# Fully filled warming products, a later first norm, weights split three pieces ahead, and last rows in two halves: a two-layer encoder on one core

## The chip, the cores and the metric

The kernel runs on one core of a Trainium2 chip. The times are device microseconds of that core for the whole kernel, one launch: the median of some runs, with the lowest and the highest. A profile is one execution of its own, taken by the hardware profiler; its span runs from its first to its last instruction or transfer, and the time of that execution is a little longer than its span.

The engines are TensorE (PE; its weight loads are listed apart as PEld), VectorE (DVE), ScalarE (ACT), GpSimd (POOL) and SyncE (SP), which only issues transfers here. Each works through its own list of instructions in order and waits on semaphores for the others. DMA transfers are issued from SP's queue and, for a few, from ACT's (ACTq in the profile).

## The reference

Two layers (DEPTH = 2) over x of 512 tokens by 1024 features, float32. Cut to what matters:

```python
for l in range(DEPTH):
    h = rms_norm(x, attn_norm_g[l])
    proj = h @ w_in[l]
    c_q, c_kv, k_rope, gq, gk, gv, pool_in, gate_logits = split_columns(proj, IN_SIZES)
    o_mla = mla_branch(c_q, c_kv, k_rope, ...)       # 8 heads, low-rank q and kv, rotary key, per-head norms
    o_gqa = gqa_branch(gq, gk, gv, ...)              # 8 heads of 64, 2 key/value heads, per-head norms, rotary
    o_pool = pool_branch(pool_in, w_pool[l], ...)    # means over 2/4/8/16 tokens minus the token, linear per group
    gates = sigmoid(gate_logits).reshape(b, s, 3, d)
    merged = (gates[:, :, 0] * (o_mla @ w_branch_mla[l])
              + gates[:, :, 1] * (o_gqa @ w_branch_gqa[l])
              + gates[:, :, 2] * (o_pool @ w_branch_pool[l]))
    x = x + merged @ w_out[l]
    hf = rms_norm(x, ffn_norm_g[l])
    u = depthwise_conv(hf @ ffn_w_up[l], ...)        # width 3, 2 x 2816 channels
    u_gate, u_val = u[..., :D_FF], u[..., D_FF:]
    x = x + (silu(u_gate) * u_val) @ ffn_w_down[l]
```

## The kernel before

**Layout and products.** Activations stand feature-major: `XM` is 128 partitions x 8 blocks (KC) x 512 tokens, the running x; `HH` and `HL` are the high and low parts of x times the norm's gain. A float32 product is made of three: high by high, high by low, low by high (`mm3`, L351 on, through the helper `mm`, L343; the profile lists nearly all products under L344). Results gather in PSUM banks with tags: two `acc`, two `ST`, two `AV`, one `mi`, one `S`. `ps(tag)` takes a bank and `free(tag)` gives it back when the evacuating operation is recorded.

**Weights.** One stream of weights comes from HBM in transfers of up to 128 x 1024 (`w_dma`, L298, on SP's queue, three raw buffers; the first eight go to general slots). Each is used in pieces of up to 512 columns. `w_split` (L305) makes a piece's high part `wh` by a copy on ACT (L208) and its low part `wl` by a subtraction (L215). Pieces 0 to 7 have that subtraction on DVE; after that `pick` (L320) takes DVE or POOL, whichever is free first by the plan. `wnext` (L336) hands out piece j and has pieces up to j + LA split first (LA = 2, `hlp` has LA + 2 buffers of each part). In `make_q` (L889 on), which takes two pieces and uses them over four token blocks, `st["la"]` cuts this to LA - 1.

**The order.** The order on each engine is written by the program itself: a `Clock` keeps a planned time, PE's work moves it forward, and `chain(...)` puts a row of steps for the other engines on a heap, each due when the one before it should end or when the key that it needs is ready. At run time each engine follows the order so recorded. In the attentions a `Filler` puts other products (gates, branch projections, `make_q`) between the score products of the heads.

**Stages of a layer.** `tok_major` makes the latents and the rotary key token-major: eight blocks by four banks by three products of 384 columns, 96 products, and consumes pieces 0 to 7 in layer 0. Then `norm_finish` (L438) sums the squares `sq` over the partitions with eight small products by `ones` into a bank `S` (in fp32, two columns each), makes the reciprocal root `rt` on DVE and POOL and the diagonal tiles `dg`; the latents' evacuation waits for `rt`. `feat_major` makes one block of 128 features by 512 tokens, 8 x 3 products; the four pooled groups come first, and after group 0 `norm_rows` (L461) spreads the norm over all partitions (`rbc`). After that follow keys and values, the two attentions, the merged branches (accumulated on DVE into `XM`, which is saved to `xsp` and loaded again), the output projection, the second norm, the feed-forward's up-projections (44 blocks) and down-projections (8 blocks of 66 products each).

**The attention's queries.** `t_pair` (L1060 on) transposes two heads into bank `mi`, then copies each head's half to `qa` (`hi`), subtracts it into the other half of `qa`, and makes a second copy `qb <- qa` of 64 x 512 (`lo`). `copy` (L470) picks ACT or DVE by the plan. The exponentials are on ACT (`ps_ST <- ps_ST`), the probabilities' parts are `ph` (a copy) and `pl` (a subtraction on DVE).

**Slots.** Nearly all other tiles of 128 x 528 floats come from one pool `sp` of 53 slots.

**Start and end.** PE begins with 18 products of `ones` by `ones`, 128 columns each (L1407). Squares of x are made by ACT (`square`) and summed by DVE (`sum_up`) beside `tok_major`. At the end, each of the eight blocks of the last down-projection is added to `XM` by DVE (128 x 512) and sent to `out` by SP.

Of the kernel before, what the change touches and what calls it, by code (L numbers as in the profile page):

```python
# [13 lines left out]
AF = mybir.ActivationFunctionType  # L14
# [4 lines left out]
P = 128  # L19
T = 512  # L20
# [8 lines left out]
SLOT = 528  # L29
NSLOT = 53  # L30
RAW = 3
# [3 lines left out]
PRE_B = 17  # L35
LA = 2
END = object()
# [209 lines left out]
def trunk(ctx: ExitStack, tc: tile.TileContext, x, w, prm, gb, cst, out):  # L247
# [8 lines left out]
    rawp = ctx.enter_context(tc.tile_pool(name="rawp", bufs=RAW))  # L256
    hlp = ctx.enter_context(tc.tile_pool(name="hlp", bufs=LA + 2))
    sp = ctx.enter_context(tc.tile_pool(name="sp", bufs=NSLOT))
# [35 lines left out]
    soff = np.concatenate([[0], np.cumsum(swidth)]) * P  # L294
    st = {"dma": 0, "split": 0, "use": 0, "la": LA}
    raws, halves = {}, {}
# [8 lines left out]
    def w_split():  # L305
        j = st["split"]
        sl, off, wd = pieces[j]
        r = raws[sl][:, off:off + wd]
        hi = hlp.tile([P, T], F32R, tag="wh", name=f"wh{j}")
        lo = hlp.tile([P, T], F32R, tag="wl", name=f"wl{j}")  # L310
        ck.fin = ck.now
        A.activation(hi[:, :wd], r, AF.Copy)
        e = V if j < KC else pick(W_BIAS, ck.fin + ck.SEM)
        ck.free[e.kind] = max(ck.free.get(e.kind, 0.0), ck.fin + ck.SEM)
        e.tensor_tensor(lo[:, :wd], r, f(hi[:, :wd]), ALU.subtract)
        done("w", j)
        halves[j] = (hi, lo)
        st["split"] += 1
# [17 lines left out]
    def wnext():  # L336
        j = st["use"]
        w_ahead(j + st["la"] if j > LA else j)
        st["use"] += 1
        need(("w", j))  # L340
        return halves.pop(j)
# [168 lines left out]
    def layer(l, sq, xsrc):  # L510
# [66 lines left out]
        tok_major(latb, 384)  # L577
        norm_finish(G1, sq, nrm)
        rt = nrm["rt"]

        def rtok(b):
            return rt[:, 2 * b:2 * b + 1]

# [15 lines left out]
        def lat_norm():  # L599
            for b in range(4):  # L600
# [3 lines left out]

        chain(*[([("rt", G1)], lambda b=b: lat_evac(b)) for b in range(4)], lat_mean,
              *rsqrt_steps(ssc.rearrange("p a b -> p (a b)"), 8, ("ssc", l)), lat_norm)

# [46 lines left out]
        for g in range(4):  # L654
            acc = ps(ptags[g])
            run(feat_major(acc, G1))
            if g == 0:
                norm_rows(G1, nrm, "acc")
            chain(*pool_steps(g, acc, ptags[g]))
# [59 lines left out]
        def gq_token():  # L719
            s_ = ssr[:, 0:32].rearrange("p (b h) -> p b h", b=4)  # L720
            V.tensor_tensor(s_, s_, bc(rt.rearrange("p (b t) -> p b t", t=2)[:, :, 0:1], [P, 4, 8]), ALU.mult)

# [166 lines left out]
        def make_q(g):  # L889
            ws = (wnext(), wnext())  # L890
            st["la"] = LA - 1
            for b in range(4):
# [8 lines left out]
                q_out(g, b, acc)  # L901
            st["la"] = LA
            if g == 1:
# [128 lines left out]
        def attention(kind, fill, okey, odst):  # L1032
# [27 lines left out]
            def t_pair(h):  # L1060
# [7 lines left out]
                for i in range(2):  # L1068
# [8 lines left out]
                    def lo(i=i, qa=qa, qb=qb, own=own, other=other):  # L1077
                        V.tensor_tensor(qa[other, :T], tp[own], f(qa[own, :T]), ALU.subtract)
                        if i == 1:
                            free("mi")  # L1080
                        copy(qb[0:64, :T], qa[own, :T], False)
                        done(*key("q", h + i))
# [290 lines left out]
        sq = None if last else slot("sq")  # L1373
        idx = 0
        for m in range(KC):
            tag = tags[m % 3]
            acc = ps(tag)
            for kc in range(FC):
# [4 lines left out]
                idx += 1  # L1383
                mm3(acc, wh[:, ws], wl[:, ws], act[kc][0][:, :T], act[kc][1][:, :T], kc == 0, kc == FC - 1)

# [19 lines left out]
    idle = ps("mi")  # L1405
    for _ in range(18):
        PE.matmul(idle[:, :P], lhsT=ones, rhs=ones, start=True, stop=True)  # L1407
    free("mi")
# [161 lines left out]
```

## Time and profile before

| | us |
|---|---|
| median of 3 runs | 1654.65 |
| lowest and highest | 1654.59, 1656.44 |
| the profiled execution | 1653.45 |
| its span | 1651.6 |
| PE busy in the span | 1643.0 (99%) |
| DVE, ACT, POOL busy | 885.7, 770.0, 929.5 |
| waits of the PE over all, by the profile | 4.5 |

How to read the profile: times are from the span's start. A row of the timeline has the start, the duration, the engine, the line of the kernel, the operation, output and inputs, shapes, a count where equal operations are joined, and in brackets how long the engine stood idle before and what ended that. A matmul's duration reaches from its start until its result is through, so that consecutive ones overlap; the pace is read from the distance of their starts. A row of the waits has the waiting operation, what it waited for, the sum of the idle time, the number of waits and the longest. A row with min/median/max gives the durations in ns of one operation by its shape.

### The profile page before, as it was taken

To read this page: it belongs to the slowest core of one execution; us is meant where nothing else is said; L and a number is where in the kernel's file an instruction comes from. 1 tells how busy PE (TensorE), PEld (TensorE's weight loads), DVE (VectorE), ACT (ScalarE), POOL (GpSimd) and SP (SyncE) were. 2 spreads that over 40 slices of the span, in tenths; PEclk is the share of its full clock that TensorE was granted. 3 is DMA by queue.
4 is the path that set the end of the run, shared out by engine and by line. 5 is a ranking of instruction groups with operands and counts; after the bars stand their busy time and mean duration, and the time that the engine had idled before them with its cause. 6 is when DMAs were issued, how large, how long until landed. Compare 5 with 4: busy or idle time off the path is not lost.

```text
span 1651.6 us, 20235 instructions
## 1 busy us (share of the span) xinstructions
PE 1643.0 (99%) x7378; PEld 1334.5 (81%) x7378; DVE 885.7 (54%) x1395; ACT 770.0 (47%) x1361; POOL 929.5 (56%) x809
## 2 busy tenths in 40 slices
PE   9999999999999999999999999999999999999999
PEld 8887887778888888888888878877788888888887
DVE  6677756643356666620046677566332666667000
ACT  6357755553444444432244577455434444444221
POOL 4762764344666566555568528634446656656543
PEclk9999999999999999999999999999999999999999
DMA  5231121124323323333333212211243223222331
GB/s 189 80 96 36 58 74 52 39 64 135 107 90 90 102 89 92 100 107 110 110 101 91 85 32 62 74 52 38 84 128 109 89 91 101 90 96 96 113 110 58
DMA packets 44595, 145.40 MB, mean 88 GB/s; under 512 B 5072, under 2 KB 6352, under 8 KB 44496
## 3 DMA queue, kind: packets, MB, share of 16 engines
q1 hardware_dynamic: 44352, 144.10, 27.7%
q8 instruction: 58, 0.95, 0.2%
q14 instruction: 41, 0.34, 0.1%
q10 hardware_dynamic: 144, 0.01, 0.0%
HBM read 139.90 MB, written 4.19 MB: 87 GB/s over the span
## 4 chain that ended last, share of the span: by engine, by line
PE 97%; DVE 1%; ACT 1%; DMA 0%; issue 0%; SPq 0%; DVEq 0%
PE ps_acc L344 43%; PE ps_AV L344 24%; PE ps_ST L344 24%; PE ps_S L344 3%; PE ps_mi L344 2%; PE ps_mi L348 1%; DVE sq L215 0%; DMA XM<-x 0%; ACT HH L208 0%; PE ps_acc L348 0%; SPq L301 0%; SPq L1410 0%; ACT wh L208 0%; DVE vmh L231 0%; DVE qa L215 0%
## 5 line engine op out<-in xcount | busy, mean ns | idle before, releaser
L215 POOL TENSOR_TENSOR wl<-raw,wh 128x512 fp32r<-128x512 f32 (+3 forms) x512 | 670.7, 1318 | 590.3 <-ACT wh L208 512.9
L208 ACT ACTIVATE wh<-raw 128x512 fp32r<-128x512 f32 (+3 forms) x522 | 314.9, 608 | 185.4 <-PE ps_ST L344 82.5
L219 DVE SCALAR_TENSOR_TENSOR a<-u,prm,a 128x512 f32<-128x512 f32 x176 | 240.6, 1368 | 79.4 <-ACT a L208 70.0
L344 PE MATMUL ps_acc<-HH,wh 128*128 128x512 f32 x592 | 234.8, 397 | 1.9 <-DVE XM L219 1.8
L344 PE MATMUL ps_acc<-HH,wl 128*128 128x512 f32 x592 | 234.2, 396 | 0.6 <-POOL wl L215 0.6
L344 PE MATMUL ps_acc<-HL,wh 128*128 128x512 f32 x592 | 233.6, 395 | 0.0
L344 PEld LDWEIGHTS ps_acc<-HH,wh 128*128 128x128 f32 x592 | 111.3, 188 | 28.5 <-ACT mqs L208 2.1
L344 PEld LDWEIGHTS ps_acc<-HH,wl 128*128 128x128 f32 x592 | 111.2, 188 | 27.9 <-POOL wl L215 1.1
L344 PEld LDWEIGHTS ps_acc<-HL,wh 128*128 128x128 f32 x592 | 111.3, 188 | 26.0
L208 ACT ACTIVATE ps_ST<-ps_ST 128x512 f32<-128x512 f32 x128 | 74.5, 582 | 115.6 <-PE ps_ST L344 115.2
L344 PE MATMUL ps_AV<-HH,wl 128*128 128x512 f32 x288 | 114.2, 397 | 0.0
L223 DVE TENSOR_REDUCE nm<-ps_S 128x1 fp32r<-128x512 f32 x128 | 87.8, 686 | 49.2 <-PE ps_S L344 48.0
L344 PE MATMUL ps_AV<-HH,wh 128*128 128x512 f32 x288 | 114.0, 396 | 0.0
L344 PE MATMUL ps_AV<-HL,wh 128*128 128x512 f32 x288 | 113.3, 393 | 0.0
L215 DVE TENSOR_TENSOR pl<-ps_ST,ph 128x512 fp32r<-128x512 f32 x128 | 87.7, 686 | 39.5 <-ACT ph L208 38.2
L215 POOL TENSOR_TENSOR al<-a,ah 128x512 fp32r<-128x512 f32 x44 | 58.1, 1321 | 84.8 <-ACT ah L208 64.6
L344 PE MATMUL ps_ST<-HH,wl 128*128 128x512 f32 x240 | 95.1, 396 | 0.0
L344 PE MATMUL ps_ST<-HH,wh 128*128 128x512 f32 x240 | 95.1, 396 | 0.0
L344 PE MATMUL ps_ST<-HL,wh 128*128 128x512 f32 x240 | 94.4, 393 | 0.0
L208 ACT ACTIVATE a<-u,prm 128x512 f32<-128x512 f32 x88 | 71.7, 815 | 31.3 <-DVE u L215 31.1
L208 ACT ACTIVATE ah<-a 128x512 fp32r<-128x512 f32 x44 | 27.8, 631 | 117.0 <-DVE u L243 111.4
L208 ACT ACTIVATE a<-a 128x512 f32<-128x512 f32 x44 | 27.8, 632 | 114.1 <-DVE u L243 114.1
(347 smaller groups left out, 3518.1 us busy)
## 6 DMA issues: line engine op xcount, KB each, us to landing
raw<-w SPq DMA_DIRECT2D x228, 512.0 KB, 3.5
raw<-w SPq DMA_DIRECT2D x13, 384.0 KB, 3.1
XM<-x SPq DMA_DIRECT2D x16, 256.0 KB, 3.9
raw<-w SPq DMA_DIRECT2D x6, 448.0 KB, 3.4
xsp<-XM SPq DMA_DIRECT2D x8, 256.0 KB, 2.0
XM<-xsp SPq DMA_DIRECT2D x8, 256.0 KB, 3.4
out<-XM SPq DMA_DIRECT2D x8, 256.0 KB, 2.0
raw<-w SPq DMA_DIRECT2D x4, 432.0 KB, 3.1
```

Of the source, the lines that this page charges most:

```text
L208: return self.eng.activation(out, in_, func, **k)
L215: return self.eng.tensor_tensor(out, *a)
L219: return self.eng.scalar_tensor_tensor(out, *a)
L223: return self.eng.tensor_reduce(out, in_, *a, **k)
L344: PE.matmul(o, lhsT=lhsT, rhs=rhs, start=start, stop=stop)
L348: PE.transpose(o, src, ident)
```

## The change

It has five parts.

1. The 18 warming products of 128 columns become 9 of 512 columns (the right operand repeats `ones` four times).
2. In layer 0 `norm_finish` and the latents' chain are recorded after the fourth of the eight blocks of pooled group 0 (12 of its 24 products), no longer ahead of it; `norm_rows` comes after group 1, no longer after group 0. Layer 1 keeps its order.
3. LA is 3: pieces are split three ahead and `hlp` has six buffers of each part. `make_q` no longer cuts this. Pieces 8, 9 and 10 have their subtraction on DVE for certain. To make room the pool of slots has 49.
4. The second copies `qb <- qa` are always on ACT.
5. In the last layer's last block of the down-projection, the 512 tokens are made in two halves of 256 columns, in banks `mi` and `S`. For the first 19 of 22 blocks both halves are computed in turn; then half 0 gets its last three blocks, its addition and its transfer (SP) are recorded, and half 1 gets its last nine products, its addition and a transfer from ACT's queue. These are 132 products of 256 columns in place of 66 of 512, two additions of 128 x 256 and two transfers of 128 KB.

```diff
--- before.py
+++ after.py
@@ -27,13 +27,13 @@
 FC = D_FF // P
 WINDOWS = (2, 4, 8, 16)
 SLOT = 528
-NSLOT = 53
+NSLOT = 49
 RAW = 3
 EXTRA = (("q", 2, (2, 5)), ("n", 2, (6, 7)), ("v", 1, (0, 3)))
 PRO = 0.47
 PRE_A = 16
 PRE_B = 17
-LA = 2
+LA = 3
 END = object()
 RSQRT_BITS = 1597463007.0
 SLACK = 35
@@ -254,7 +254,7 @@
 
     cp = ctx.enter_context(tc.tile_pool(name="cp", bufs=1))
     rawp = ctx.enter_context(tc.tile_pool(name="rawp", bufs=RAW))
-    hlp = ctx.enter_context(tc.tile_pool(name="hlp", bufs=LA + 2))
+    hlp = ctx.enter_context(tc.tile_pool(name="hlp", bufs=LA + 3))
     sp = ctx.enter_context(tc.tile_pool(name="sp", bufs=NSLOT))
     sm = ctx.enter_context(tc.tile_pool(name="sm", bufs=2))
     pp = ctx.enter_context(tc.tile_pool(name="pp", bufs=1, space=PSUM))
@@ -292,7 +292,7 @@
 
     pieces, swidth = _stream()
     soff = np.concatenate([[0], np.cumsum(swidth)]) * P
-    st = {"dma": 0, "split": 0, "use": 0, "la": LA}
+    st = {"dma": 0, "split": 0, "use": 0}
     raws, halves = {}, {}
 
     def w_dma():
@@ -310,7 +310,7 @@
         lo = hlp.tile([P, T], F32R, tag="wl", name=f"wl{j}")
         ck.fin = ck.now
         A.activation(hi[:, :wd], r, AF.Copy)
-        e = V if j < KC else pick(W_BIAS, ck.fin + ck.SEM)
+        e = V if j < KC + 3 else pick(W_BIAS, ck.fin + ck.SEM)
         ck.free[e.kind] = max(ck.free.get(e.kind, 0.0), ck.fin + ck.SEM)
         e.tensor_tensor(lo[:, :wd], r, f(hi[:, :wd]), ALU.subtract)
         done("w", j)
@@ -335,7 +335,7 @@
 
     def wnext():
         j = st["use"]
-        w_ahead(j + st["la"] if j > LA else j)
+        w_ahead(j + LA if j > LA else j)
         st["use"] += 1
         need(("w", j))
         return halves.pop(j)
@@ -575,11 +575,11 @@
         ltags = ("acc", "acc", "ST", "ST")
         latb = [ps(t) for t in ltags]
         tok_major(latb, 384)
-        norm_finish(G1, sq, nrm)
-        rt = nrm["rt"]
+        if l:
+            norm_finish(G1, sq, nrm)
 
         def rtok(b):
-            return rt[:, 2 * b:2 * b + 1]
+            return nrm["rt"][:, 2 * b:2 * b + 1]
 
         mx = [slot("mx") for _ in range(4)]
         ssc = small("ssc", [P, 4, 2])
@@ -602,8 +602,12 @@
                 V.tensor_scalar(mx[b][:, 256:384], mx[b][:, 256:384], ssc[:, b, 1:2], None, ALU.mult)
             done("lat", l)
 
-        chain(*[([("rt", G1)], lambda b=b: lat_evac(b)) for b in range(4)], lat_mean,
-              *rsqrt_steps(ssc.rearrange("p a b -> p (a b)"), 8, ("ssc", l)), lat_norm)
+        def latents():
+            chain(*[([("rt", G1)], lambda b=b: lat_evac(b)) for b in range(4)], lat_mean,
+                  *rsqrt_steps(ssc.rearrange("p a b -> p (a b)"), 8, ("ssc", l)), lat_norm)
+
+        if l:
+            latents()
 
 
         mixed = {}
@@ -653,8 +657,11 @@
         ptags = ("AV", "AV", "mi", "S")
         for g in range(4):
             acc = ps(ptags[g])
-            run(feat_major(acc, G1))
-            if g == 0:
+            for n, _ in enumerate(feat_major(acc, G1)):
+                if l == 0 and g == 0 and n == 3:
+                    norm_finish(G1, sq, nrm)
+                    latents()
+            if g == (l == 0):
                 norm_rows(G1, nrm, "acc")
             chain(*pool_steps(g, acc, ptags[g]))
 
@@ -718,7 +725,7 @@
 
         def gq_token():
             s_ = ssr[:, 0:32].rearrange("p (b h) -> p b h", b=4)
-            V.tensor_tensor(s_, s_, bc(rt.rearrange("p (b t) -> p b t", t=2)[:, :, 0:1], [P, 4, 8]), ALU.mult)
+            V.tensor_tensor(s_, s_, bc(nrm["rt"].rearrange("p (b t) -> p b t", t=2)[:, :, 0:1], [P, 4, 8]), ALU.mult)
 
         def gq_norm(b):
             o = gqo[b][:, :T].rearrange("p (h f) -> p h f", f=64)
@@ -888,7 +895,6 @@
 
         def make_q(g):
             ws = (wnext(), wnext())
-            st["la"] = LA - 1
             for b in range(4):
                 if b:
                     yield
@@ -899,7 +905,6 @@
                     lh, ll = lat[kc]
                     mm3(acc[:, :384], lh[:, bs], ll[:, bs], wh[:, :384], wl[:, :384], kc == 0, kc == 1)
                 q_out(g, b, acc)
-            st["la"] = LA
             if g == 1:
                 chain(([("ssq", l, i, b) for i in range(2) for b in range(4)],
                        lambda: G.tensor_scalar(ss[:, 0], ss[:, 0], 1.0 / 96, EPS, ALU.mult, ALU.add)),
@@ -1078,7 +1083,7 @@
                         V.tensor_tensor(qa[other, :T], tp[own], f(qa[own, :T]), ALU.subtract)
                         if i == 1:
                             free("mi")
-                        copy(qb[0:64, :T], qa[own, :T], False)
+                        A.activation(qb[0:64, :T], qa[own, :T], AF.Copy)
                         done(*key("q", h + i))
 
                     steps.append((hi, lo))
@@ -1371,7 +1376,18 @@
 
         last = l == L - 1
         sq = None if last else slot("sq")
-        idx = 0
+        idx, tail = 0, []
+        two = [ps(t) for t in ("mi", "S")] if last else None
+
+        def half(n, kc, wh, wl):
+            ts = slice(256 * n, 256 * n + 256)
+            mm3(two[n][:, :256], wh, wl, act[kc][0][:, ts], act[kc][1][:, ts], kc == 0, kc == FC - 1)
+
+        def out_half(n):
+            ts = slice(256 * n, 256 * n + 256)
+            V.tensor_tensor(XM[:, KC - 1, ts], two[n][:, :256], XM[:, KC - 1, ts], ALU.add)
+            (SY, nc.scalar)[n].dma_start(out[KC - 1][:, ts], XM[:, KC - 1, ts])
+
         for m in range(KC):
             tag = tags[m % 3]
             acc = ps(tag)
@@ -1381,7 +1397,20 @@
                 need(("act", l, kc))
                 ws = slice((idx % 4) * P, (idx % 4) * P + P)
                 idx += 1
-                mm3(acc, wh[:, ws], wl[:, ws], act[kc][0][:, :T], act[kc][1][:, :T], kc == 0, kc == FC - 1)
+                if not (last and m == KC - 1):
+                    mm3(acc, wh[:, ws], wl[:, ws], act[kc][0][:, :T], act[kc][1][:, :T], kc == 0, kc == FC - 1)
+                elif kc < FC - 3:
+                    half(0, kc, wh[:, ws], wl[:, ws])
+                    half(1, kc, wh[:, ws], wl[:, ws])
+                else:
+                    half(0, kc, wh[:, ws], wl[:, ws])
+                    tail.append((kc, wh[:, ws], wl[:, ws]))
+            if tail:
+                chain(lambda: out_half(0))
+                for z in tail:
+                    half(1, *z)
+                chain(lambda: out_half(1))
+                continue
 
             def resid(m=m, acc=acc, tag=tag):
                 V.tensor_tensor(XM[:, m, :], acc, XM[:, m, :], ALU.add)
@@ -1403,8 +1432,8 @@
     A.activation(warm, warm, AF.Exp)
     V.memset(f(ones), 1.0)
     idle = ps("mi")
-    for _ in range(18):
-        PE.matmul(idle[:, :P], lhsT=ones, rhs=ones, start=True, stop=True)
+    for _ in range(9):
+        PE.matmul(idle, lhsT=ones, rhs=ones[:, None, :].to_broadcast([P, 4, P]), start=True, stop=True)
     free("mi")
     for kc in range(KC):
         SY.dma_start(XM[:, kc, :], x[kc])
```

## The prediction

> **What bounds the kernel now.** I read the page first, then the PE's waits, then the timeline around every place where the PE stood still. The page (busy us, share of the span, instructions; then the chain that ended last) and, as third line, the last row of the chain's own list (start, us, engine, tile, count):
>
> ```profile
> PE 1643.0 (99%) x7378; PEld 1334.5 (81%) x7378; DVE 885.7 (54%) x1395; ACT 770.0 (47%) x1361; POOL 929.5 (56%) x809
> PE 97%; DVE 1%; ACT 1%; DMA 0%; issue 0%; SPq 0%; DVEq 0%
> 1632.54 15.29 PE ps_ST L344 x66
> ```
>
> TensorE is busy 99% of the span and makes 97% of the chain; a product of 512 columns costs 15.29 / 66 = 0.232 us. Nothing in the change takes products away, so it can only win what the PE loses at the start, in its waits and at the end. All its waits:
>
> ```profile
> PE ps_acc L344 <- DVE XM L219: 1.8, 1, 1.8
> PE ps_mi L1407 <- DVE ones L243: 1.1, 1, 1.1
> PE ps_acc L344 <- POOL wl L215: 0.6, 1, 0.6
> PE ps_S L344 <- DVE sq L215: 0.6, 1, 0.6
> PE ps_acc L344 <- DVE vml L215: 0.4, 2, 0.2
> ```
>
> Behind the first 1.1 us (nothing to multiply yet) stand 3.4 us; with what each stop adds on both sides it is some 5 us. So the ceiling of the whole change is about 5 us, plus the slow clock at the start, plus what the tail gives.
>
> The profiled execution took 1653.45 us (span 1651.6 and 1.85 around it); the median of the runs is 1654.65. I sum against 1653.45 and add the 1.2 at the end.
>
> **1. Start: dense warming and the first norm.** The PE's timeline (start, us, operation, idle before):
>
> ```profile
> 1.10 4.11 PE L1407 MATMUL ps_mi<-ones 128*128 128x128 f32 x18 [1.10 <-DVE ones L243]
> 5.01 0.63 PE L344 MATMUL ps_acc<-wh,HH 128*128 128x384 f32 x1
> 5.76 0.69 PE L344 MATMUL ps_acc<-wl,HH 128*128 128x384 f32 x1
> 6.25 0.52 PE L344 MATMUL ps_acc<-wh,HL 128*128 128x384 f32 x1
> ...
> 9.45 0.52 PE L344 MATMUL ps_acc<-wh,HH 128*128 128x384 f32 x1
> ...
> 10.22 0.34 PE L344 MATMUL ps_acc<-wh,HH 128*128 128x384 f32 x1
> ...
> 24.09 0.34 PE L344 MATMUL ps_ST<-wh,HL 128*128 128x384 f32 x1
> 25.02 1.05 PE L344 MATMUL ps_S<-ones,sq 128*128 128x2 f32 x8 [0.60 <-DVE sq L215]
> 25.94 0.48 PE L344 MATMUL ps_AV<-HH,wh 128*128 128x512 f32 x1
> ```
>
> From 6.25 to 9.45 there are ten steps of 0.320; from 10.22 (16th of 96 matmuls) to 24.09 (the last) 80 steps of 0.1734. So the clock came near 9.8, and each earlier matmul costs 0.147 us too much. The 18 warming matmuls run 0.228 apart (4.11 / 18) for 128 columns; a cold 384-column one needs 0.320, so 128 columns would be 0.107, and the array was under half filled. Nine of 512 columns at 0.427 (0.320 x 4/3) make 3.84 us without gaps, 1.10 to 4.94, so the first real product stays at 5.0.
>
> Does that bring the clock sooner? Before, it came 3.6 us after 6.25, where the stream becomes gapless. The same count from 1.10 gives 4.7; if the gaps at 5.3 to 6.25 spoil it, nothing changes. I take the middle, 6.4: the eleven matmuls of 6.25 to 9.45 win 11 x 0.147 = 1.6 us.
>
> [...]
>
> Now the norm. The PE was through with the 96 at 24.26 and stood until 25.02 for the squares, 0.76 lost; 12 product matmuls (0.232 each, 2.8 us) now come first. With the clock at 6.4 it asks for the squares at 24.26 - 1.6 + 2.8 = 25.45, and without an earlier clock at 27.1. Who is then late? The sum of squares:
>
> ```profile
> 17.30 0.68 DVE L215 TENSOR_TENSOR sq<-sq,sqt 128x512 f32<-128x512 f32 x1
> 18.37 6.59 DVE L215 TENSOR_TENSOR sq<-sq,sqt 128x512 f32<-128x512 f32 x5
> 21.01 1.71 POOL L215 TENSOR_TENSOR wl<-raw,wh 128x512 fp32r<-128x512 f32 x1 [0.79 <-ACT wh L208]
> ```
>
> Five additions took 6.59 instead of 3.4, with POOL's weight splits beside them. The change puts the low halves of pieces 8 to 10 between these additions on DVE (3 x 0.68, as an addition of this size) and POOL's 11 to 13 after them. That is 18.37 + 3.4 + 2.0 = 23.8 undisturbed; three POOL splits cost 3.2 before, 1.07 each, so two in the way make 25.9 and three 27.0. The wait left is 0 to 1.6; I take two, 0.5, as the disturbance shows in the row. Start: -0.76 - 1.6 + 0.5 = **-1.9**; ends -0.7 (no earlier clock, or an earlier one that the squares eat) and -2.8 (clock before 5.0, 2.0 won, no wait). The latents and the pooled rows fall 2.8 later than before relative to the products; three and a half more product groups (24 x 0.232 = 5.6 us each, 19 us) cover them, so I price that at nothing, and at up to 0.5 (inside the small waits of 4) if that cover is gone.
>
> **2. The stop in layer 0 (second copies).** PE and DVE around it:
>
> ```profile
> 151.77 0.34 PE L344 MATMUL ps_acc<-wh,ctl 128*128 128x384 f32 x1
> 153.94 0.47 PE L344 MATMUL ps_acc<-HH,wh 128*128 128x512 f32 x1 [1.83 <-DVE XM L219]
> 149.84 0.69 DVE L231 CAST ph<-ps_ST 128x512 fp32r<-128x512 f32 x1 [0.32 <-ACT ps_ST L208]
> 151.29 0.68 DVE L215 TENSOR_TENSOR qa<-ps_mi,qa 64x512 fp32r<-64x512 f32 x1
> 151.99 1.21 DVE L231 CAST qb<-qa 64x512 fp32r<-64x512 f32 x1
> 153.12 0.67 DVE L219 SCALAR_TENSOR_TENSOR XM<-gt,ps_acc 128x512 f32<-128x512 f32 x1
> ```
>
> The next product was due at 151.94 and ran at 153.94: 2.0 lost, because the accumulator is freed by XM (153.12 to 153.79), in line on DVE behind a second copy of 1.21. How many such copies does the edit move?
>
> ```profile
> L208 ACT ACTIVATE qb<-qa x15: 617/629/632, 106.0 to 1001.3; 64x512 fp32r<-64x512 f32 x15
> L231 DVE CAST qb<-qa x1: 1208/1208/1208, 152.0 to 152.0; 64x512 fp32r<-64x512 f32 x1
> ```
>
> One of sixteen, and it is this one (ACT pays 0.63). In the built order `ph` goes to ACT too (-0.69), but a copy of `qa` (0.69) comes to DVE ahead of XM: net 1.21 less on DVE. But `pl` now waits for `ph` behind other work on ACT, for which I allow 0.5. **-0.7**: XM ends near 153.1. Ends: -0.3 (ACT later still) and -1.7 (nothing in line). Late next is XM itself, still 1.2 us behind the 151.94.
>
> **3. The stop in layer 1 (three pieces ahead).**
>
> ```profile
> 971.75 0.33 PE L344 MATMUL ps_acc<-wh,ctl 128*128 128x384 f32 x1
> 972.20 0.49 PE L344 MATMUL ps_acc<-HH,wh 128*128 128x512 f32 x1
> ...
> 973.55 0.50 PE L344 MATMUL ps_acc<-HH,wl 128*128 128x512 f32 x1 [0.64 <-POOL wl L215]
> 974.11 0.50 PE L344 MATMUL ps_S<-ka,qa 128*128 128x512 f32 x1
> ```
>
> Unhindered, the score product would start at 971.92 + 3 x 0.23 = 972.6; it started at 974.11, 1.5 lost, 1.1 of it on a weight piece just split. This lies in `make_q`, where the look-ahead was cut to one piece; now three are ready, so the split is out of the path. The last 0.3 waited for the query; in the built order nine more products (3 x 0.232 + 6 x 0.173, 1.7 us) stand between the transposes that make it and the score product, so it should be in time. **-1.4**; ends -0.8 (the query or the deeper queue on POOL stays late) and -1.5.
>
> **4. New places with little slack.** With the other order the four small transposes (103.86 to 104.22) no longer stand between these products and the one that needs XM:
>
> ```profile
> 103.01 0.69 DVE L219 SCALAR_TENSOR_TENSOR XM<-gt,ps_acc 128x512 f32<-128x512 f32 x1 [0.77 <-PE ps_acc L344]
> 103.86 0.60 PE L348 MATMUL ps_mi<-C,gqr 128*128 128x128 f32 x4
> 104.22 0.48 PE L344 MATMUL ps_acc<-HH,wh 128*128 128x512 f32 x1
> ```
>
> XM ends at 103.70, the product is now due at 103.86: 0.16 us to spare, the same in layer 1. The four slots less and the deeper splitting (ACT, POOL and SP issue the same splits and loads, only one piece sooner) may add waits too. **+0.4**; ends 0 and +1.5 (about one more stop of 0.35 in each layer, and two of 0.4 elsewhere). The two waits for `vml` stay.
>
> **5. Tail: the last rows in halves.**
>
> ```profile
> 216.58 0.28 PE L344 MATMUL ps_acc<-wh,cth 128*128 128x256 f32 x1
> ...
> 217.28 0.40 PE L344 MATMUL ps_acc<-HH,wh 128*128 128x512 f32 x1
> 1647.86 0.69 DVE L215 TENSOR_TENSOR XM<-ps_ST,XM 128x512 f32<-128x512 f32 x1 [14.58 <-PE ps_ST L344]
> 1648.58 0.34 SPq L1389 DMA_DIRECT2D out<-XM  x1
> ```
>
> Six matmuls of 256 columns go from 216.58 to 217.28, 0.117 each; 132 of them are 15.4 against 15.29, +0.1 (six are few: with an allowance of 0.008 each +1.1). [...]
>
> Half 0 is added and sent while the last nine matmuls (1.05 us) run. The addition behind the end shrinks from 0.69 to about 0.41 (half its columns, bounded by 0.35 and 0.69): -0.3. From the issue at 1648.58 to the end are 3.05 us; a half transfer, sent by ACT's queue instead of SP's, may save nothing or a quarter of that (half the bytes, were half of it transfer), 0.8; I take 0.2, nearer to nothing, since the rows do not divide it. **-0.4**; ends +0.8 and -1.1.
>
> **Sum.** -1.9 - 0.7 - 1.4 + 0.4 - 0.4 = -4.0: 1653.45 becomes 1649.45, and the median 1650.7. All good ends together: -7.1, 1647.6; all bad ends: -0.7 - 0.3 - 0.8 + 1.5 + 0.8 = +0.5, 1655.2.
>
> **The rivals.** A measurement of this kernel tells about 0.2% from no change, 3.3 us, so faster begins below 1651.3.
> - A, the clock comes no sooner (for: the gaps at 5.3 to 6.25 stay; against: the row of half-filled warming). Then the start gives only -0.76 and the sum is -2.9: 1651.8. [...]
> - B, everything opens: clock near 4.7, squares in time, both stops gone: -2.6 - 1.5 - 1.5 - 0.7 = -6.3, 1648.4. For it: no wait of the PE besides those listed; against: XM in layer 0 is still 1.2 behind.
> - C, the stops move on: XM and the query stay late, and the narrow places of 4 open: -1.9 - 0.3 - 0.8 + 1.5 - 0.4 = -1.9, 1652.8. For it: the margin of 0.16; against: the DVE lines there get shorter.
> - D, slower: 49 slots. In the attentions each head asks for slots in turn; with four less, a writer on ACT or DVE waits for an earlier tile's last reader, and the exponential behind it comes late. Price: 32 heads (two branches, eight heads, two layers); from 0.23 us each it eats the 4.0 and 3.3 beyond. With 0.6 (the POOL wait above) at every second head it is +9.6: 1660.3. For it:
>
> ```profile
> 127.00:154.00 27.00, 25.17 (x114) 19.72 (x112) 21.53 (x33) 20.61 (x37) 8.27 (x7) 1.00 0.12 35
> ```
>
> In this window of an attention (us, then busy PE, PEld, DVE, ACT, POOL) DVE and ACT are 80% and 76% busy. Against it: what is left, 5 to 6 us in 27, and no wait of the PE on a slot now.
>
> **How the numbers follow.** Forecast 0.48 (own range 1649.2 to 1652.1, about 0.7 of it under 1651.3), A 0.16, B 0.14, C 0.11, D 0.11. Faster: 0.34 + 0.14 + a third of A = 0.54; slower: D, 0.11; the rest, 0.35, within 0.2%. The range 1647.6 to 1655.2 holds all but D and a little beyond B.
>
> **What would show it.** The first 0.17 us step in the timeline: near 6.4 right, near 9.8 is A, before 5 is B. The wait of `ps_S` for `sq`: about 0.5. The stop at 152 shorter but there, the one at 972 gone, no wait for `wl`. The last 132 matmuls in 15.4 us, the end 2.8 us behind the last issue. New waits of the PE over 0.5 us in the attentions, spread over the heads, would make the prediction wrong (D); so would a start that loses in the squares what it wins in clock.

## The result and the profile after

The changed kernel takes 1649.21 us (median of 6 runs, 1648.48 to 1649.44) against 1654.76 before (6 runs, 1654.59 to 1656.44): a ratio of 0.9964, 95% interval 0.9951 to 0.9977, so about 5.5 us less. The forecast was 1650.7, faster by 4.0. Its profiled execution took 1649.25 us, 4.2 less than the one before (1653.45), and that is the first thing to notice: profile against profile the gain is 4.2, median against median 5.55.

The page after (busy us, share, instructions), and its chain:

```profile
PE 1640.4 (100%) x7435; PEld 1336.7 (81%) x7435; DVE 890.5 (54%) x1404; ACT 761.8 (46%) x1357; POOL 921.9 (56%) x805
PE 98%; DVE 1%; ACT 1%; DMA 0%; SPq 0%; issue 0%
```

All waits of the PE in it (the operation, what it waited for, us in total, times, longest):

```profile
PE ps_acc L344 <- DVE XM L219: 1.4, 1, 1.4
PE ps_mi L1436 <- DVE ones L243: 1.1, 1, 1.1
PE ps_S L344 <- DVE sq L215: 0.6, 1, 0.6
PE ps_acc L344 <- DVE vml L215: 0.4, 2, 0.2
PE ps_acc L344 <- DVE wl L215: 0.2, 1, 0.2
```

The wait for POOL's `wl` is gone, the one for XM went from 1.8 to 1.4, the one for the squares is as long as before. No new wait over 0.25 us has come. Where each part stands, on the PE's timeline of the changed kernel, first the start:

```profile
1.10 4.21 PE L1436 MATMUL ps_mi<-ones 128*128 128x512 f32 x9 [1.10 <-DVE ones L243]
5.11 0.52 PE L344 MATMUL ps_acc<-wh,HH 128*128 128x384 f32 x1
5.79 0.45 PE L344 MATMUL ps_acc<-wl,HH 128*128 128x384 f32 x1 [0.16 <-DVE wl L215]
6.08 0.34 PE L344 MATMUL ps_acc<-wh,HL 128*128 128x384 f32 x1
6.25 0.34 PE L344 MATMUL ps_acc<-wh,HH 128*128 128x384 f32 x1
...
25.17 0.40 PE L344 MATMUL ps_AV<-HH,wl 128*128 128x512 f32 x1
26.18 1.05 PE L344 MATMUL ps_S<-ones,sq 128*128 128x2 f32 x8 [0.61 <-DVE sq L215]
27.09 0.48 PE L344 MATMUL ps_AV<-HH,wh 128*128 128x512 f32 x1
```

The step of 0.17 us stands at 6.08 instead of near 10: the clock came 4 us sooner (the records of the clock have the grant at 5.74, before at 9.98). The PE now asks for the squares at 25.40 (25.17 + 0.23) and still stands until 26.18. At 27.09 it goes on with 12 pooled products done, where before it stood at 25.94 with none: 25.94 - (27.09 - 12 x 0.232) = 1.63 us won.

The stop of layer 0, on PE and DVE:

```profile
150.00 0.34 PE L344 MATMUL ps_acc<-wh,ctl 128*128 128x384 f32 x1
151.78 0.47 PE L344 MATMUL ps_acc<-HH,wh 128*128 128x512 f32 x1 [1.44 <-DVE XM L219]
148.04 0.69 DVE L231 CAST qa<-ps_mi 64x512 fp32r<-64x512 f32 x1 [0.71 <-ACT qa L208]
150.94 0.69 DVE L219 SCALAR_TENSOR_TENSOR XM<-gt,ps_acc 128x512 f32<-128x512 f32 x1
```

It lasts 1.6 us (150.17 to 151.78) instead of 2.0. The copy of 1.21 is no longer ahead of XM, but another one of 0.69 is (of `qa`), and DVE idled 0.71 before it.

The stop of layer 1 is not there any more; the products follow each other without a pause:

```profile
971.52 0.34 PE L344 MATMUL ps_acc<-wh,ctl 128*128 128x384 f32 x1
971.70 0.40 PE L344 MATMUL ps_acc<-HH,wh 128*128 128x512 f32 x1
971.93 0.40 PE L344 MATMUL ps_acc<-HL,wh 128*128 128x512 f32 x1
```

And the end:

```profile
1643.85 0.28 PE L344 MATMUL ps_S<-ah,wl 128*128 128x256 f32 x1
1644.16 0.42 DVE L215 TENSOR_TENSOR XM<-ps_S,XM 128x256 f32<-128x256 f32 x1 [0.64 <-PE ps_S L344]
1644.62 0.35 ACTq L1389 DMA_DIRECT2D out<-XM x1
```

From the start of the last product to the end of the span (1647.3) are 3.47 us, before 4.20 (1647.42 to 1651.63). The 132 halves started 0.118 apart, so they took 15.56 in place of 15.27. The addition gave 0.27 of the difference, the way from the issue to the end 0.35 (2.70 instead of 3.05). From the first of these products to the end are 18.91 us, before 19.24: 0.34 less.

Sum of the places: 1.63 + 0.4 + 1.5 + 0.34 = 3.9 of the 4.3 us by which the span is shorter; the rest is spread over small steps of about 0.1.

### The profile page after: what moved, and what is told of

Its sections match the earlier page's. It is cut to its first block, busy times and chain, and to the rows that moved or that the text cites. A ratio compares the mean times of both kernels' runs of the same rounds, so it can differ in the third digit from the quotient of the medians.

```text
span 1647.3 us, 20363 instructions
## 1 busy us (share of the span) xinstructions
PE 1640.4 (100%) x7435; PEld 1336.7 (81%) x7435; DVE 890.5 (54%) x1404; ACT 761.8 (46%) x1357; POOL 921.9 (56%) x805
## 4 chain that ended last, share of the span: by engine, by line
PE 98%; DVE 1%; ACT 1%; DMA 0%; SPq 0%; issue 0%
PE ps_acc L344 44%; PE ps_AV L344 24%; PE ps_ST L344 23%; PE ps_S L344 4%; PE ps_mi L344 2%; PE ps_mi L348 1%; DVE sq L215 0%; DMA XM<-x 0%; ACT wh L208 0%; ACT sqt L208 0%; DVE wl L215 0%; PE ps_acc L348 0%; SPq L301 0%; ACT HH L208 0%; SPq L1439 0%
## 5 line engine op out<-in xcount | busy, mean ns | idle before, releaser
L215 POOL TENSOR_TENSOR wl<-raw,wh 128x512 fp32r<-128x512 f32 (+2 forms) x508 | 662.9, 1315 | 589.0 <-ACT wh L208 457.7
L208 ACT ACTIVATE wh<-raw 128x512 fp32r<-128x512 f32 (+3 forms) x522 | 308.8, 607 | 125.6 <-PE ps_ST L344 41.1
```

The source lines that it names most:

```text
L208: return self.eng.activation(out, in_, func, **k)
L215: return self.eng.tensor_tensor(out, *a)
```

## The experiments

### The start: each part undone by itself

Dense warming undone:

```diff
-    for _ in range(9):
-        PE.matmul(idle, lhsT=ones, rhs=ones[:, None, :].to_broadcast([P, 4, P]), start=True, stop=True)
+    for _ in range(18):
+        PE.matmul(idle[:, :P], lhsT=ones, rhs=ones, start=True, stop=True)
```

> The changed kernel with the 18 half-filled warming products back. Theory (dense warming brings the clock; only what the squares leave of it counts): the first 0.173 us step of the 384-column products falls between 9.5 and 13.1 instead of near 6.1, the PE asks for the squares at 27.1 to 28.5 and does not wait for them (they are ready at 26.1), so the start loses 0.9 to 2.4 us against the changed kernel: median 1650.1 to 1651.6. Rival (the phase of the clock is chance, the kind of warming does not matter): first fast step near 6 also here, loss under 0.3 us, median 1649.2 to 1649.5.

Measured: 1649.98 us (6 runs, 1649.63 to 1650.20), 0.77 more than the changed kernel, span 1648.3 against 1647.3. The clock came at 10.4 and the PE did not wait for the squares. So the theory holds, a little under its lower end. The dense warming is worth 0.8 us here and not the 2.0 by which it brings the PE to the squares sooner (25.40 instead of 27.36), since the PE then waits 0.8 for them; of the remaining 1.2 the spans show 0.94.

The norm back in front of the pooled products, dense warming kept (part 2 undone):

```diff
-        if l:
-            norm_finish(G1, sq, nrm)
+        norm_finish(G1, sq, nrm)
...
-        if l:
-            latents()
+        latents()
...
-                if l == 0 and g == 0 and n == 3:
-                    norm_finish(G1, sq, nrm)
-                    latents()
-            if g == (l == 0):
+                pass
+            if g == 0:
```

> The changed kernel with the first norm back in front of the pooled products, dense warming kept. Theory: the PE is through with the 96 products near 22.6 and stands until the squares are summed, near 26 (two to three and a half us idle), so the start loses 2.0 to 2.8 us: median 1651.2 to 1652.0. Rival (the squares come earlier when the PE asks earlier): idle under 1.5 us, loss under 1 us, median under 1650.2.

Measured: 1653.88 us (11 runs, 1651.64 to 1656.34), 4.7 more than the changed kernel: more than the theory's 2.0 to 2.8. The PE's wait is what was expected; its timeline in this run:

```profile
22.55 0.34 PE L344 MATMUL ps_ST<-wh,HL 128*128 128x384 f32 x1
25.03 1.05 PE L344 MATMUL ps_S<-ones,sq 128*128 128x2 f32 x8 [2.14 <-DVE sq L215]
25.94 0.48 PE L344 MATMUL ps_AV<-HH,wh 128*128 128x512 f32 x1
26.26 0.56 PE L344 MATMUL ps_AV<-HL,wh 128*128 128x512 f32 x1
26.62 0.63 PE L344 MATMUL ps_AV<-HH,wl 128*128 128x512 f32 x1
```

The last row has what nobody had put on paper: a 512-column product of 0.63 where 0.40 is usual. Behind the stop the slow clock is back. Its records show it withdrawn from 26.34 to 29.75. Ten of the eleven runs have a mean granted clock under 1.000, so a withdrawal somewhere; the one that has not took 1651.64 us, 2.4 more than the changed kernel, which is inside the theory's 2.0 to 2.8. So the wait was priced rightly, and the withdrawal comes on top.

Both undone (both edits above):

> The changed kernel with both parts of the start undone. Theory (the two parts only pay together): loss of 1.3 to 2.4 us against the changed kernel, no more than with the norm alone undone: median 1650.5 to 1651.6. Rival (each part pays for itself): the losses of the two single undoings add up to 3 us or more, median above 1652.2.

Measured: 1652.20 us (11 runs, 1651.42 to 1656.03), 3.0 more. The theory's sum is too small (1.3 to 2.4), and the rival's median (above 1652.2) is just not reached; the single losses do add up to more, 0.8 + 4.7. With the norm in front, dense warming makes the median 1.7 us worse. That is the clock: here 5 of 11 runs have a mean under 1.000, there 10 of 11. Where the clock was held, the two differ little (1651.42 to 1652.20 here, 1651.64 there). In this trace too the clock was withdrawn, at 26.0.

The kernel before, once more:

> The kernel before, once more, for its trace. [...] Rival (the clock always comes near 9.8): the same start, and the 1.2 us between the profiled execution and the median lie elsewhere.

Measured: median 1655.64 (10 runs, 1652.53 to 1659.05), profiled execution 1656.49, span 1654.7. The first fast step is at 9.31, sooner than in the first profile (10.05), and yet the span is 3.1 longer. Of the rival, the same start is not there, but its second half holds: the difference lies elsewhere. The clock is the cause in another way. Windows of this trace (from:to, us, then busy us of PE, PEld, DVE, ACT and POOL with their instructions, the granted clock, and DMA):

```profile
22.85:26.26 3.41, 2.40 (x16) 2.06 (x16) 2.16 (x3) 0.63 (x1) 1.59 (x1) 1.00 0.52 154
26.26:29.68 3.42, 3.42 (x9) 2.65 (x8) 1.63 (x4) 1.59 (x6) 2.89 (x2) 0.50 0.00 0
152.55:155.97 3.42, 1.58 (x9) 1.20 (x8) 3.34 (x5) 3.02 (x6) 2.87 (x3) 1.00 0.12 19
155.97:159.38 3.41, 3.41 (x10) 2.53 (x9) 1.26 (x3) 1.18 (x2) 1.06 (x1) 0.50 0.35 139
```

Behind the stop for the squares and behind the stop of layer 0 the clock ran at 0.50 for 3.41 us each time, so that each stop cost another 1.7 us: 3.4 in all, and the span is 3.1 longer than in the first profile (1654.7 against 1651.6), where neither happened. The 28 runs of the kernel before that were timed beside these four experiments fall into steps by their mean clock:

```
mean clock   runs   us                  withdrawals
1.000         8     1653.25 to 1653.95  0
0.999        12     1654.27 to 1655.38  1
0.998         7     1656.32 to 1656.84  2
0.997         1     1659.10             3
```

One withdrawal as in these rows takes 3.41 x 0.5 / 1651 = 0.001 from the mean clock, which is the step of the first column; the last column gives their number by that. It is a reading of rounded means, but the times have gaps at the same places. The medians of the steps are 1653.6, 1654.8, 1656.6 and 1659.1: 1.2, 1.8 and 2.5 apart, about the 1.7 of a withdrawal, which the runs do not give more closely. By its time the median of before has one withdrawal in it, the first profile had none; the six runs of the changed kernel and the six with the old warming have a mean of 1.000 each.

### Where the clock was withdrawn

In the changed kernel 40 gaps were put into the PE's stream, in both up-projections:

```diff
                 up_evac(c, part, acc, tag)
+                if part == 1 and c >= 2:
+                    pb = ps("S")
+                    PE.matmul(pb, lhsT=ones, rhs=ones[:, None, :].to_broadcast([P, 4, P]), start=True, stop=True)
+                    for w_ in GAPS[(c - 2) % len(GAPS)]:
+                        nc.scalar.activation(pb[:, :w_], pb[:, :w_], AF.Copy)
+                    PE.matmul(pb[:, 0:2], lhsT=f(ones), rhs=f(ones[:, 0:2]), start=True, stop=True)
+                    free("S")
```

> The changed kernel with 40 gaps put into the PE's stream, behind the second product block of a channel group in both up-projections (one product of ones, one to four in-place copies of 128 to 512 columns on ACT, one product of two columns; the PE is idle 1.0 to 3.5 us each time). [...]

Measured (one execution): the gaps came out shorter than meant, at 0.84 to 2.52 us (from 0.23 behind the start of the product of ones to the start of the next). There are six withdrawals, all behind the six gaps of 1.80 us, none behind the sixteen of 1.91 to 2.52 or the shorter ones. So stops well under 3.41 us were enough here, and the length of a gap did not decide alone: no gap over 1.9 lost the clock and those of 1.80 did. For the 3.41 us ahead of a withdrawal, and for as long a stretch over a stop behind which the clock stayed, I summed the columns that streamed through the PE, at 0.1734 us for 384 of them (the pace at the full clock):

```
share of the 3.41 us    kernel and start of the stretch
0.09                    norm first 22.92                        clock withdrawn after it
0.25                    queries on ACT (below) 25.01            withdrawn
0.37                    gaps 529.78                             withdrawn
0.37, 0.385             before again 22.85, 152.55              withdrawn
0.40                    both undone 22.59                       withdrawn
0.48                    first profile of before 23.63           kept
0.50                    changed 149.10                          kept
```

Two stretches of the run with gaps, and what follows them:

```profile
529.78:533.20 3.42, 1.78 (x10) 1.16 (x9) 0.75 (x2) 2.76 (x6) 0.72 (x1) 1.00 0.30 121
533.20:536.61 3.41, 3.41 (x10) 2.63 (x9) 3.34 (x3) 0.42 (x1) 2.25 (x2) 0.50 0.12 17
1536.70:1540.12 3.42, 1.86 (x9) 1.58 (x10) 0.64 (x1) 3.21 (x6) 1.30 (x2) 1.00 0.00 0
1540.12:1543.53 3.41, 3.41 (x17) 2.73 (x16) 2.93 (x5) 0.40 (x1) 1.71 (x2) 1.00 0.47 154
```

The first had 0.37 of its time streaming and lost the clock, the second kept it. The time that the profile counts as busy does not sort them: the stretch at 22.85 was busy for 2.40 us of 3.41 and lost the clock, the one at 1536.70 for 1.86 and kept it (the eight small products by `ones` count as busy, but stream two columns each). Nor does the length of a stop: the one of 2.0 us in layer 0 (151.94 to 153.94 in the first profile of before), as long as the one from 153.40 to 155.41 in the kernel before again, was followed by a granted clock of 1.00 (153.34 to 156.75). A stop of 2.0 us that lies whole in such a stretch leaves 0.385 (152.55 above), one of 1.6 leaves 0.50 (149.10 in the changed kernel). In the six runs of the changed kernel the mean clock stayed at 1.000. So the small gain at the stop of layer 0 may have been worth more than its 0.4; that is my estimate from these shares, and no run shows it by itself.

### Part 3 alone, part 4 alone, part 5 alone, on the kernel before

Part 3:

```diff
-NSLOT = 53
+NSLOT = 49
-LA = 2
+LA = 3
-    hlp = ctx.enter_context(tc.tile_pool(name="hlp", bufs=LA + 2))
+    hlp = ctx.enter_context(tc.tile_pool(name="hlp", bufs=LA + 3))
-        e = V if j < KC else pick(W_BIAS, ck.fin + ck.SEM)
+        e = V if j < KC + 3 else pick(W_BIAS, ck.fin + ck.SEM)
-        w_ahead(j + st["la"] if j > LA else j)
+        w_ahead(j + LA if j > LA else j)
-            st["la"] = LA - 1
...
```

> The kernel before with part 3 alone (three pieces ahead, six buffers, 49 slots, low halves of pieces 8 to 10 on DVE). Theory: the stop of layer 1 near 972 (1.5 us) is gone with its wait for wl, the one of layer 0 near 152 stays at 1.6 to 2.1, and no new wait of the PE over 0.5 us appears; where the clock is held, the span is 1649.8 to 1650.6. Rival D of the prediction (49 slots make the writers wait): new waits of the PE in the attentions, summing to 3 us or more.

Measured: 1652.18 us (10 runs, 1651.72 to 1654.29), span of the profile 1649.7. No stop is left near 972, the one near 152 is 1.6 us, and no new wait has come. So 49 slots cost nothing that shows, and the prediction's slower case is out. The span is just under the expected range. One thing more stands in this trace: without part 4, all sixteen second copies are already on ACT (before, fifteen were).

```profile
L208 ACT ACTIVATE qb<-qa x16: 613/630/634, 106.0 to 1000.2; 64x512 fp32r<-64x512 f32 x16
```

So the other order that comes with part 3 moves the copy of 1.21 by itself, and the stop is as long as in the changed kernel, which has part 4 too.

Part 4:

```diff
-                        copy(qb[0:64, :T], qa[own, :T], False)
+                        A.activation(qb[0:64, :T], qa[own, :T], AF.Copy)
```

> The kernel before with part 4 alone (second copies on ACT). Theory: one copy moves, the stop of layer 0 shrinks from 2.0 to between 1.2 and 1.7 us, that of layer 1 stays at 1.5, and the clock is no longer withdrawn behind the stop of layer 0; where the clock is held, the span is 1650.9 to 1651.3. Rival (the gain in layer 0 came from the other order of three pieces ahead): the stop stays at 2.0.

Measured: 1652.72 us (10 runs, 1651.99 to 1654.45), span 1650.6. The stop near 152 is:

```profile
152.62 0.47 PE L344 MATMUL ps_acc<-HH,wh 128*128 128x512 f32 x1 [0.73 <-DVE XM L219]
```

0.9 us, shorter than expected and shorter than the 1.6 of the changed kernel, with 0.35 lost behind it around the score product at 155.02. The span is just under the expected range. The stop of layer 1 stayed at 1.5. Its trace has no withdrawal; four of its ten runs have a mean clock under 1.000, which the squares can bring about alone (with part 3 alone two of ten, in the kernel before beside them 18 of 24). So moving one copy of 1.21 us off DVE gives 0.76 by itself (from 151.55 to 155.83 in 4.28 us, the same products before in 5.04), and the rival falls for this kernel. In the changed kernel it is the rival that holds: part 3 alone moves the copy and brings the stop to 1.6, and with part 4 it is 1.6 too. The order of part 3 puts a copy of `qa` on DVE (148.04 above), which part 4 alone does not have. No run has the changed kernel without part 4.

Part 5 (the lines of the diff from `two = ...` to `continue`):

```diff
+        two = [ps(t) for t in ("mi", "S")] if last else None
...
+            if tail:
+                chain(lambda: out_half(0))
+                for z in tail:
+                    half(1, *z)
+                chain(lambda: out_half(1))
+                continue
```

> The kernel before with part 5 alone (last rows in halves). Theory: from the first of the last 132 products to the end of the span 18.6 to 18.9 us instead of 19.1, everything else as before. Rival (halves cost more in products than the shorter addition and transfer give): 19.1 or more.

Measured: 1654.71 us (10 runs) against 1654.62 for the kernel before beside it (24 runs): in the medians nothing; the withdrawals, by the mean clock in eight of its ten runs, scatter them by far more than 0.3. In the trace, from the first of the last 132 products to the end, 18.97 against 19.24: 0.3 less, though just over the expected 18.6 to 18.9.

### A version that is faster still

What stood on the changed kernel's timeline at 26.18 and 151.78 suggests two edits. They ran on another chip than the experiments above; the kernel before took 1654.36 us beside them (9 runs), 0.4 less than beside the changed kernel, so a difference of some tenths from 1649.21 says nothing. First, the first copies of the queries on ACT too:

```diff
-                        copy(qa[own, :T], tp[own])
+                        A.activation(qa[own, :T], tp[own], AF.Copy)
```

> The changed kernel with the first copies of the queries on ACT too, so that DVE no longer waits for ACT ahead of XM in the stop of layer 0. Theory (what is left of that stop is DVE's line: a copy of 0.69 behind a wait of 0.71): the stop falls from 1.6 to 0.2 to 0.6 us, median 1647.9 to 1648.4. Rival (ACT's line becomes the bound there): stop over 1.2, median 1649 or more.

Measured: 1649.71 us (5 runs, 1648.29 to 1651.10). The stop fell from 1.6 to 0.63, about as expected, so DVE's line was what was left of it; but the median did not follow, though two of the five runs lie in the expected range. In this execution, the slowest, the squares were late:

```profile
21.82 4.95 DVE L215 TENSOR_TENSOR sq<-sq,sqt 128x512 f32<-128x512 f32 x4
26.82 1.05 PE L344 MATMUL ps_S<-ones,sq 128*128 128x2 f32 x8 [1.39 <-DVE sq L215]
```

The last additions began 0.64 later than in the changed kernel (21.18), the PE asked 0.13 sooner (25.27), and so it stood 1.6 us; the 3.41 us ahead of the withdrawal (first row) had streamed for a quarter:

```profile
25.01:28.42 3.41, 2.02 (x13) 1.51 (x12) 1.85 (x4) 0.00 (x0) 0.26 (x1) 1.00 0.28 115
28.42:31.84 3.42, 3.42 (x10) 2.67 (x9) 1.94 (x7) 1.94 (x7) 2.73 (x3) 0.50 0.00 0
```

The clock had come at 4.5 here, but that is not the cause: in the run with gaps, which has the changed kernel's start, it came at 4.1, and the PE asked at 25.37 and was served at 26.17, as in the changed kernel. What made the squares late here, and what held up the other two runs over the range, no trace shows.

Second, the low halves of pieces 11 and 12 on DVE:

```diff
-        e = V if j < KC + 3 else pick(W_BIAS, ck.fin + ck.SEM)
+        e = V if j < KC + 5 else pick(W_BIAS, ck.fin + ck.SEM)
```

> The changed kernel with the low halves of pieces 11 and 12 on DVE as well, so that POOL does nothing beside the sum of squares. Theory (POOL's splits stretch the additions): the four last additions take 2.5 to 3 us instead of 4.94 plus at most one subtraction of 0.69 in front, the wait of the PE for the squares falls from 0.6 (0.79 lost) to under 0.2, median 1648.4 to 1648.8. Rival (the squares are late by their own line): wait of 0.5 or more, median unchanged.

Measured: 1649.02 us (5 runs, 1648.85 to 1649.33). The wait for the squares is gone, since the additions are no longer stretched; DVE's rows of this run and that of the changed kernel:

```profile
20.75 1.42 DVE L215 TENSOR_TENSOR sq<-sq,sqt 128x512 f32<-128x512 f32 x2
22.08 0.69 DVE L215 TENSOR_TENSOR wl<-raw,wh 128x512 fp32r<-128x512 f32 x1
22.68 1.42 DVE L215 TENSOR_TENSOR sq<-sq,sqt 128x512 f32<-128x512 f32 x2
```

```profile
21.18 4.94 DVE L215 TENSOR_TENSOR sq<-sq,sqt 128x512 f32<-128x512 f32 x4
```

Four additions take 2.84 instead of 4.94. But the median is only 0.2 lower, less than the 0.4 to 0.8 expected. In the trace the gain is there, and more: behind the norm the PE goes on at 26.25 instead of 27.09, 0.85 ahead. At the end it is 0.34 ahead. The order of the products is the same, and the 0.5 between are lost in small steps over the whole run, for a reason that no run shows.

Both edits:

> Both edits on the changed kernel. Theory: the gains add, 1.6 to 2.1 us in all, median 1647.1 to 1647.7.

Measured: 1647.92 us (4 runs, 1647.64 to 1647.96), a ratio to the kernel before of 0.9958 (0.9941 to 0.9975). That is 1.3 less than the changed kernel, under the expected 1.6 to 2.1, and the fastest of this study. In the trace the gains do add: it is about 2.0 ahead of the changed kernel at 157 us and 1.6 at the end. Its clock came at 4.5 as in the first edit's run, and here the PE met the squares ready and nothing was withdrawn (mean clock 1.000). Its waits:

```profile
PE ps_mi L1436 <- DVE ones L243: 1.1, 1, 1.1
PE ps_acc L344 <- DVE XM L219: 0.4, 1, 0.4
PE ps_acc L344 <- DVE vml L215: 0.4, 2, 0.2
PE ps_acc L344 <- DVE wl L215: 0.4, 1, 0.4
```

## Why the prediction was right, and where it was off

The direction and the range held (1649.21 in 1647.6 to 1655.2). The likeliest value was 1.5 us too high. Step by step:

- **The bound.** Right: the PE's waits, the slow start and the tail held all of the gain.
- **Start, -1.9.** Measured -1.63. The clock came at 5.7 instead of 6.4, a bit more than taken; the squares ate more (0.78 instead of 0.5). The half-filled products run 0.213 apart, not 0.228 (the 4.11 us of their row reach to the last result), so by the 0.107 estimated for 128 columns the array was half filled and not under half; nothing in the sum rests on that. The 6.4 was a choice, and the 2.0 of the good end, for a clock before 5.0, an estimate; no run shows either as taken: dense warming had the clock at 4.1 to 6.4 in six traces, and what an earlier one gave went into the wait for the squares. The undoings bear out that the two parts belong together: without dense warming no wait for the squares, and without the later norm a wait of 2.1.
- **Layer 0, -0.7.** Measured -0.4, within its ends. The number is near, but the part is the wrong one: the term is put down to part 4, and the order of part 3 moves the copy without it. By itself, on the kernel before, part 4 is worth 0.76. With part 3, 0.8 of the 1.21 taken off DVE came back in its other waits, where 0.5 was allowed for.
- **Layer 1, -1.4.** Measured -1.5; part 3 alone removes the stop.
- **New narrow places, +0.4.** Mis-sized: no such wait came. The place with 0.16 us to spare (near 102 now) held, and the slots cost nothing.
- **Tail, -0.4.** Measured -0.34. The products cost +0.3 instead of +0.1 (0.118 each over 132, where six had shown 0.117), and what lies behind the last product gave 0.73 instead of 0.5 (the transfer 0.35 of it, taken for 0.2).
- **"I sum against 1653.45 and add the 1.2 at the end."** This is the step that failed. The sum itself, -4.0, is almost the -4.2 between the two profiled executions. The 1.2 was taken for a constant offset between a profile and the other runs. The runs show it is a withdrawn clock: by its time one withdrawal (3.41 us at 0.50) in the median run of before (the step from none to one is 1.2 in the medians), none in the first profile, none in the runs of the changed kernel. A sum over waits could not see that, but the runs could: 1654.59 to 1656.44 was a spread of 1.9 us in a kernel whose stops sum to 5.
- **The rivals.** A, C and D did not come. B gave 1648.4, the stops fully open; the changed kernel is not there, as the stop of layer 0 stayed, and came near it for another reason. The more that B and the start's good end won by a clock before 5 would not have come: with the clock at 4.1 (run with gaps) the PE asked for the squares at 25.37, with 5.7 at 25.40.

That the norm's move removes the withdrawals at the squares is shown for two pairs of kernels that differ in it alone (by the mean clock, none in six runs and 10 of 11 with dense warming, none in six and 5 of 11 with the old). It is no guard by itself: in the changed kernel's trace the PE still streamed next to nothing from 25.40 to 27.09, as long as in the first profile (24.26 to 25.94), and with squares later by 0.64 the first of the two edits above lost the clock there. That the shorter stop of layer 0 removes the others rests on the shares above, 0.50 of 3.41 us with a stop of 1.6 and 0.385 with one of 2.0 behind which the clock went; the first profile kept its clock behind the same 2.0, so this is an estimate. The runs of parts 3 and 4 alone, with both a shorter stop and the old start, point the same way (6 of 20 under a mean clock of 1.000, against 18 of 24), but they do not say at which stop a run lost it, and part 3 also moves splits to DVE beside the squares.

## What to carry to other kernels

A stop of the PE had two prices in this kernel: its length and, in part of the runs (by the mean clock 20 of 28 of the kernel before had one somewhere), 3.41 us at 0.50 of the clock behind it, another 1.7 us; so 0.4 us off a stop of 2 us could be worth more than 0.4. Before summing against one profile, look whether the runs lie in steps, and what the profile's own run had of them. And an earlier clock was worth nothing by itself where the next thing was late: it had to be moved together with what the PE then waited for, or the stop grew (2.1 us instead of 1.0) and the clock went again more often (10 of 11 runs with dense warming and the norm in front, 5 of 11 with the old warming). When two edits touch one plan, look at each one's trace alone: one of them may already do what the other is credited with.

## What the runs showed of the hardware

The full clock of TensorE was withdrawn eleven times in the traces of this study, for 3.41 us at 0.50 where the rows show it. Products had streamed for 0.09 to 0.40 of the 3.41 us ahead in the six cases counted above, and for 0.48 and 0.50 in the two stretches behind which it stayed. Stops of 1.8 to 3.2 us were enough (with the small products by `ones` counted in), and stops of the same length were also passed at the full clock: 2.0 us in the first profile of the kernel before, and sixteen gaps of 1.91 to 2.52.

With 18 half-filled warming products (128 columns every 0.213 us) the first grant came at 8.9 to 10.4 us in seven traces; with nine dense ones (512 columns every 0.427 us) at 4.1 to 6.4 in six. That the count of columns is what decides, of the grant or of a withdrawal, and not something that goes with it, no run here separates.
